# Low halves of 40 weight units: from a VectorE subtraction to a ScalarE negation plus an accumulating DMA

## The chip, the core and the metric

The kernel runs on one core of a Trainium2 chip. The metric is the device time of one execution in microseconds; lower is better. TensorE (PE) multiplies matrices, ScalarE (ACT) and VectorE (DVE) work elementwise, GpSimd (POOL) does a little arithmetic and issues some DMAs, SyncE (SP) issues the weight loads.

## The reference, cut to what matters

Two transformer-like layers over 256 tokens of width 2048, all in float32. The first is attention (differential attention and retention), cross-attention over a memory of 256 tokens and a gated feed-forward; the second is a hybrid of windowed attention and pooling. Nearly all work is in products of a 256-row activation with large weights:

```python
proj = h @ w_in[l]                       # 2048 x 7168
dq, dk, dv, rq, rk, rv, rg = split_cols(proj)
...
x = x + mixed @ w_o[l]
xq = (hx @ w_xq[l]); xk = (hm @ w_xk[l]); xv = (hm @ w_xv[l])
x = x + xo @ w_xo[l]
x = x + (jax.nn.silu(hf @ w_gate[l]) * (hf @ w_up[l])) @ w_down[l]
```

## The kernel before

**Units.** Every weight matrix is read once, as a stream of 128x1024 float32 tiles (512 KB), called `raw`. One such tile is one unit of a product (a few later ones are cut smaller). A product keeps float32 accuracy by splitting each operand into two parts: `hi`, the value rounded to the type that TensorE multiplies in one pass (float32r), and `lo`, the rest. A product is then made of three, hi·hi, hi·lo and lo·hi. `split_to` (L379 to L382) makes the two parts of a weight unit: ScalarE casts `raw` to `hi` (L381), VectorE subtracts, `lo = raw - hi` (L382).

**Matmuls.** There are two shapes of product. In layout "R" (`gemm_1k`) a unit holds one slice of 128 rows of the weight and is the moving operand: 12 matmuls with 512 columns each (L348, L349, L350), the second of which reads `lo`. In layout "T" (`gemm`) a unit holds two slices of 512 columns and is the stationary operand: 8 pairs of matmuls (L283 and L284, both through L353), the second of each pair reading `lo`. TensorE executes its matmuls in the order of the program.

**The stream.** `emit_items` walks a list of items made by `plan`. For a unit it takes a `hi` and a `lo` buffer (4 of each, `SPL_BUFS`), splits the unit, and then issues the load of the raw tile that comes six tiles later into the buffer just read (`RAW_BUFS = 6`, issued by SP at L230). `next_unit` is called ahead of the matmuls of unit u and emits the splits up to unit u + 3 (`LOOK = 3`); ahead of the last unit of a product it looks only two ahead, and `look_ahead` makes up for it in the middle of the evacuation. So the cast of unit u + 3 takes the buffer of unit u - 1, and can start when TensorE is done with unit u - 1. All engines work through their own instructions in the order of the program, so a cast also stands behind the ScalarE work that was emitted before it.

**Around it.** Between units `tick` emits one step of small jobs: softmax heads, transposes, evacuations. On POOL these are the power functions of the norms (L361) and the loads of the memory (L799).

**The stretch that the change touches** runs from the product `rv` (the retention values) to `xv1` (the last product of the cross-attention's values): rv, rg, o0, o1 (layout R, 16 units each), xk and xq in two halves each (layout T, 64 units), xv0 and xv1 (layout R, 16 each). That is 160 units, all 128x1024.

Of the kernel before, what the change touches and what calls it, by code (L numbers as in the profile page):

```python
# [9 lines left out]
F32 = mybir.dt.float32  # L10
F32R = mybir.dt.float32r
AF = mybir.ActivationFunctionType
ALU = mybir.AluOpType
# [106 lines left out]
class Builder:  # L120
# [113 lines left out]
    def emit_items(self, upto):  # L234
        while self.next_item <= min(upto, len(self.items) - 1):
            i = self.next_item
            job, c0, n, fn = self.items[i]
            raw = self.raw[job][:, c0 : c0 + n]
            if fn:
                fn(raw)  # L240
            else:
                hi = self.wpool.tile([P, n], F32R, tag="hi", name=f"hi{i}", bufs=SPL_BUFS)
                lo = self.wpool.tile([P, n], F32R, tag="lo", name=f"lo{i}", bufs=SPL_BUFS)
                for c in range(0, n, 256 if i == 0 else n):
                    w = slice(c, c + (256 if i == 0 else n))
                    self.split_to(raw[:, w], hi[:, w], lo[:, w])
                self.units[i] = (hi, lo)
            self.next_item += 1
            if c0 + n == 1024:
                del self.raw[job]  # L250
                self.emit_dma()
# [279 lines left out]
    def build(self):  # L531
        a = self.a
        w_in, w2 = a["w_in"][0], a["w_in_2"][0]
        G = {}

        def group(name, w, c0, ncol=1024, k0=0, nkt=KT, unit=None):
            G[name] = Gemm(name, w, k0, nkt, c0, ncol, unit or ncol)
            order.append(G[name])

        def wide(name, w, c0, ncol=1024, k0=0, nkt=KT):  # L540
            for i in range(ncol // 512):
                group(f"{name}.{i}", w, c0 + i * 512, 512, k0, nkt, 1024)

        order = []
        group("dq", w_in, 0)
        wide("dk", w_in, 1024)
        group("dv", w_in, 2048)
        wide("rqk", w_in, 3072)
        group("rv", w_in, 4096)
        group("rg", w_in, 5120)  # L550
        for c in range(2):
            group(f"o{c}", a["w_o"][0], c * 1024)
        for c in range(2):
            for n in ("xk", "xq"):
                wide(f"{n}{c}", a[f"w_{n}"][0], c * 1024)
        for n in ("xv", "xo"):
            for c in range(2):
                group(f"{n}{c}", a[f"w_{n}"][0], c * 1024)
        parts = ((0, 16), (16, 16), (32, 12))
        self.ff = []  # L560
        for pi, (k0, nk) in enumerate(parts):
            for i in range(nk // 4):
                for n in ("gate", "up"):
                    group(f"{n[0]}{pi}{i}", a[f"w_{n}"][0], (k0 + 4 * i) * P, 512, unit=1024)
            for c0, n in DOWN_COLS[pi == 2]:
                group(f"d{pi}{c0}", a["w_down"][0], c0, n, k0, nk)
            self.ff.append(nk)
        group("pu", w2, 2560)
        wide("gp", w2, 3584)
        wide("q", w2, 0)  # L570
        wide("kv", w2, 1024, 512)
        for c in range(4):
            if c == 2:
                wide("ga", w2, 1536)
            wide(f"m{c}", a["w_merge_2"][0], c * 1024)
        for c in range(4):
            wide(f"ba{c}", a["w_branch_attn_2"][0], c * 512, 512, 0, 8)
            wide(f"bp{c}", a["w_branch_pool_2"][0], c * 512, 512, 0, 8)
        for c0, n in OUT_COLS:
            group(f"out{c0}", a["w_out_2"][0], c0, n)  # L580

        ada = a["w_ada_2"][0]
        extras, todo = {}, []
        for k in range(KT):
            for c in range(0, 3 * D, 1024):
                src = ada[k * P : k * P + P, c : c + 1024].rearrange("p (b c) -> p b c", b=1)
                todo.append((src, self.ada_item(k, c)))
        hosts = []
        for g in order:
            if g.name[:2] in ("g0", "u0", "g1", "u1") or g.name in ("g20", "u20"):  # L590
                hosts += [(g.name, j) for j in HOST_W]
            elif g.name[:2] in ("d0", "d1"):
                hosts += [(g.name, j) for j in HOST_R]
        for i, ex in enumerate(todo):
            extras[hosts[i + 4]] = [ex]
        hosts = [(n, j) for n, js in SHIFT_HOSTS for j in js]
        for k in range(KT):
            extras[hosts[k]] = [(G["pu"].src[k], self.shift_item(k))]
        wp = a["w_pool_group_2"][0].rearrange("g (b p) d -> p (g b) d", p=P)
        for i in range(2):  # L600
            extras[("gp.0", 3 + i)] = [(wp[:, 4 * i : 4 * i + 4, :], self.pool_item(i))]
        wo = a["w_out_2"][0][:, OUT_REST:].rearrange("(k p) c -> p k c", p=P)
        for i in range(4):
            extras[("out0", 8 + 2 * i)] = [(wo[:, 4 * i : 4 * i + 4, :], self.out_item(i))]
        self.plan(order, extras)

        self.block1(G)
        self.ffn(G)
        self.block2(G)
        assert self.unit_no == len(self.unit_item)  # L610
        self.es.close()
# [1014 lines left out]
```

## Time and profile before

| | |
|---|---|
| time, median of 2 runs | 2114.75 us (2112.83 to 2116.67) |
| time of the profiled execution | 2116.45 us |
| its span (first to last instruction of the program) | 2114.6 us |
| PE busy | 2102.7 us, 99% |
| DVE busy | 1398.5 us, 66% |
| ACT busy | 1052.1 us, 50% |
| POOL busy | 80.9 us, 4% |
| bytes moved by DMA | 453.54 MB, mean 214 GB/s |

The span is what the profiler saw of the program; the time of the same execution is 1.85 us longer. Busy times are shares of the span. In the rows below, L381 is line 381 of the kernel; `out<-in` names tiles with their buffer numbers left out.

### The profile page before, as it was taken

Reading aid. Unit: us, or ns where it says so; the run is one execution under the profiler, and the core shown is the slowest. Engines: PE = TensorE matmul, PEld = TensorE weight load, DVE = VectorE, ACT = ScalarE, POOL = GpSimd, SP = SyncE. Lnnn points to the kernel's source line nnn. Section 1 sums busy time; section 2 is a strip of 40 time slices with the busy share of each in tenths; the row PEclk is TensorE's granted clock in tenths of the full one; section 3 lists DMA queues with packets and bytes.
Section 4 is the critical chain, followed back from the end, with each engine's and each line's share of the span. In section 5 each row is a group of like instructions: output and inputs, shape, how many; then the busy total and the mean of one; then the engine's idle time right before and its main releaser. Section 6 shows DMA issues by size and latency. Waiting matters only on the chain.

```text
span 2114.6 us, 30084 instructions
## 1 busy us (share of the span) xinstructions
PE 2102.7 (99%) x11582; PEld 1821.0 (86%) x11582; DVE 1398.5 (66%) x1762; ACT 1052.1 (50%) x1598; POOL 80.9 (4%) x97
## 2 busy tenths in 40 slices
PE   9999999999999999999999999999999999999998
PEld 9888888888888888888888888888898988888887
DVE  5556655665555557787777777877876766546764
ACT  5454555565444455444344443444755554655543
POOL 0200010000000000000000000000000000001300
PEclk9999999999999999999999999999999999999999
DMA  7755556555655567888888887768866556565562
GB/s 261 213 193 172 184 165 203 186 170 169 201 168 169 170 188 248 292 274 295 265 278 288 268 304 257 257 195 304 267 191 188 185 174 188 173 191 177 185 234 90
DMA packets 188527, 453.54 MB, mean 214 GB/s; under 512 B 14742, under 2 KB 23264, under 8 KB 188128
## 3 DMA queue, kind: packets, MB, share of 16 engines
q1 hardware_dynamic: 184992, 441.58, 64.3%
q0 software_dynamic: 3392, 10.06, 1.5%
q8 instruction: 90, 1.47, 0.3%
q14 instruction: 53, 0.43, 0.1%
HBM read 449.46 MB, written 4.22 MB: 215 GB/s over the span
## 4 chain that ended last, share of the span: by engine, by line
PE 98%; DMA 0%; issue 0%; DVE 0%; SPq 0%; ACT 0%; DVEq 0%; POOLq 0%; POOL 0%; ACTq 0%
PE acc L353 56%; PE acc L349 13%; PE acc L348 13%; PE acc L350 13%; PE m L353 1%; PE m L390 1%; PE m L349 1%; PE m L350 1%; PE m L348 1%; DMA raw<-in_w_in 0%; PE m L972 0%; PE m L1217 0%; DVE S L1342 0%; PE m L921 0%; SPq L228 0%
## 5 line engine op out<-in xcount | busy, mean ns | idle before, releaser
L382 DVE TENSOR_TENSOR lo<-raw,hi 128x1024 fp32r<-128x1024 f32 (+2 forms) x751 | 880.6, 1183 | 486.6 <-ACT hi L381 484.2
L353 PE MATMUL acc<-S,hi 128*128 128x512 f32 x3360 | 1186.4, 397 | 0.0
L381 ACT CAST hi<-raw 128x1024 fp32r<-128x1024 f32 (+2 forms) x751 | 748.0, 1010 | 526.9 <-PE acc L350 228.7
L353 PE MATMUL acc<-S,lo 128*128 128x256 f32 x3360 | 941.4, 280 | 0.0
L353 PEld LDWEIGHTS acc<-S,hi 128*128 128x128 f32 x3360 | 630.7, 188 | 150.3 <-issue 0.9
L353 PEld LDWEIGHTS acc<-S,lo 128*128 128x128 f32 x3360 | 634.4, 189 | 0.3
L348 PE MATMUL acc<-hi,S 128*128 128x512 f32 (+1 forms) x1088 | 422.1, 388 | 0.0
L349 PE MATMUL acc<-lo,S 128*128 128x512 f32 (+1 forms) x1088 | 417.0, 383 | 0.3 <-DVE lo L382 0.3
L350 PE MATMUL acc<-hi,S 128*128 128x512 f32 (+1 forms) x1088 | 417.3, 384 | 0.0
L350 PEld LDWEIGHTS acc<-hi,S 128*128 128x128 f32 x1088 | 204.4, 188 | 40.8
L349 PEld LDWEIGHTS acc<-lo,S 128*128 128x128 f32 x1088 | 204.6, 188 | 38.7 <-DVE lo L382 0.6
L348 PEld LDWEIGHTS acc<-hi,S 128*128 128x128 f32 x1088 | 204.5, 188 | 38.8
L343 DVE TENSOR_TENSOR S<-acc,S 128x256 f32<-128x256 f32 x136 | 54.0, 420 | 60.4 <-ACT S L342 60.3
L342 ACT COPY S<-acc 128x256 f32<-128x256 f32 x136 | 47.2, 377 | 85.4 <-PE acc L353 85.4
L624 DVE SCALAR_TENSOR_TENSOR S<-raw,ccol,S 128x1024 f32<-128x1024 f32 x60 | 76.7, 1278 | 0.0
L348 PE MATMUL acc<-S,hi 128*128 128x256 f32 x256 | 73.4, 287 | 0.6 <-ACT hi L381 0.6
L350 PE MATMUL acc<-S,lo 128*128 128x256 f32 x256 | 72.6, 284 | 0.9 <-DVE lo L382 0.9
L349 PE MATMUL acc<-S,hi 128*128 128x256 f32 x256 | 72.6, 284 | 0.4 <-DVE S L394 0.4
L350 PEld LDWEIGHTS acc<-S,lo 128*128 128x128 f32 x256 | 49.0, 192 | 1.3 <-DVE lo L382 1.3
L348 PEld LDWEIGHTS acc<-S,hi 128*128 128x128 f32 x256 | 49.1, 192 | 0.8 <-ACT hi L381 0.7
L349 PEld LDWEIGHTS acc<-S,hi 128*128 128x128 f32 x256 | 49.1, 192 | 0.7 <-DVE S L394 0.6
L381 ACT CAST S<-S 128x512 fp32r<-128x512 f32 x34 | 21.1, 621 | 50.5 <-DVE S L1050 48.5
(286 smaller groups left out, 1145.6 us busy)
## 6 DMA issues: line engine op xcount, KB each, us to landing
raw<-in_w_in SPq DMA_DIRECT2D x183, 512.0 KB, 4.4
raw<-in_w_ada SPq DMA_DIRECT2D x96, 512.0 KB, 4.7
raw<-in_w_gate SPq DMA_DIRECT2D x88, 512.0 KB, 4.9
raw<-in_w_up SPq DMA_DIRECT2D x88, 512.0 KB, 4.8
raw<-in_w_down SPq DMA_DIRECT2D x88, 512.0 KB, 5.5
raw<-in_w_merge SPq DMA_DIRECT2D x64, 512.0 KB, 4.3
raw<-in_w_o SPq DMA_DIRECT2D x32, 512.0 KB, 4.1
raw<-in_w_xk SPq DMA_DIRECT2D x32, 512.0 KB, 4.2
```

The costliest lines, as they stand in the source:

```text
L342: self.nc.scalar.copy(dst, bank[:, 1, :])
L343: self.nc.vector.tensor_tensor(dst, bank[:, 0, :], dst, op=ALU.add)
L348: mm(o, sh, mh, start=first, stop=False, skip_group_check=True)
L349: mm(o, sh, ml, start=False, stop=False, skip_group_check=True)
L350: mm(o, sl, mh, start=False, stop=last, skip_group_check=True)
L353: self.nc.tensor.matmul(o, l, r, start=start, stop=stop, skip_group_check=True)
L381: self.nc.scalar.copy(hi, src)
L382: self.nc.vector.tensor_tensor(lo, src, hi.bitcast(F32), op=ALU.subtract)
L390: nc.tensor.transpose(ps[:, i, t * P : t * P + P], rows(t)[:, i * P : i * P + P], self.ident)
L624: nc.vector.scalar_tensor_tensor(acc, raw, ck, acc, op0=ALU.mult, op1=ALU.add)
```

## The change

For every fourth item from the first unit of `rv` up to, and not including, the first of `xo0`, `lo` is made in another way. ScalarE casts `raw` to `hi` as before, then ScalarE writes `-hi` into `lo`, and then a DMA issued from POOL adds `raw` to `lo` in place. No other items lie in this part of the list, so these are 160 / 4 = 40 units. The VectorE subtraction of these units goes. The `raw` buffer of such a unit is read last by the DMA, and TensorE reads `lo` after the DMA has landed.

```diff
@@ emit_items
-                for c in range(0, n, 256 if i == 0 else n):
-                    w = slice(c, c + (256 if i == 0 else n))
-                    self.split_to(raw[:, w], hi[:, w], lo[:, w])
+                if i in self.added:
+                    self.nc.scalar.copy(hi, raw)
+                    self.nc.scalar.activation(lo, hi.bitcast(F32), AF.Copy, scale=-1.0)
+                    self.nc.gpsimd.dma_start(lo.bitcast(F32), raw, accum_op=ALU.add)
+                else:
+                    for c in range(0, n, 256 if i == 0 else n):
+                        w = slice(c, c + (256 if i == 0 else n))
+                        self.split_to(raw[:, w], hi[:, w], lo[:, w])
@@ build, after self.plan(order, extras)
+        first = self.unit_item[self.unit_name.index("rv")]
+        last = self.unit_item[self.unit_name.index("xo0")]
+        self.added = set(range(first, last, 4))
```

## Rows read from the trace of the kernel before

**Rows 1.** The page, part 1: busy us (share of the span) xinstructions.
```profile
PE 2102.7 (99%) x11582; PEld 1821.0 (86%) x11582; DVE 1398.5 (66%) x1762; ACT 1052.1 (50%) x1598; POOL 80.9 (4%) x97
```

**Rows 2.** The page, part 4: the chain that ended last, by engine.
```profile
PE 98%; DMA 0%; issue 0%; DVE 0%; SPq 0%; ACT 0%; DVEq 0%; POOLq 0%; POOL 0%; ACTq 0%
```

**Rows 3.** Busy time by stretch of the span, for the changed stretch.
```profile
core 0: us, PE busy (x) PEld busy (x) DVE busy (x) ACT busy (x) POOL busy (x), PEclk, DMA share, GB/s
...
201.43:674.59 473.16, 472.95 (x2451) 403.12 (x2449) 275.72 (x376) 243.58 (x399) 14.25 (x16) 1.00 0.56 178
```

**Rows 4.** The view of waits, PE alone, from 201 to 675 us.
```profile
PE m L862 <- DVE C L857: 0.2, 1, 0.2
```

**Rows 5.** Groups by line and shape: busy us, mean ns | idle before.
```profile
L382 DVE TENSOR_TENSOR lo<-raw,hi 128x1024 fp32r<-128x1024 f32 x691 | 845.8, 1234 | 470.2 <-ACT hi L381 467.7
...
L381 ACT CAST hi<-raw 128x512 fp32r<-128x512 f32 x40 | 24.2, 618 | 15.0 <-DVE lo L382 7.4 <-PE acc L350 6.3 <-DVE XR L1203 0.8
...
L512 ACT ACTIVATE J<-XR 128x512 f32<-128x512 f32 x24 | 15.2, 633 | 0.2
```

**Rows 6.** Groups by line, ACT alone, from 190 to 675 us.
```profile
L381 ACT CAST hi<-raw 128x1024 fp32r<-128x1024 f32 x161 | 166.9, 1050 | 102.5 <-PE acc L350 61.0 <-PE acc L353 38.7 <-issue 1.4
```

**Rows 7.** Timeline, ACT and PE (start us, us): cast of a unit, matmul reading its lo.
```profile
192.03 1.05 ACT L381 CAST hi<-raw 128x1024 fp32r<-128x1024 f32 x1 [1.72 <-PE acc L353]
201.85 0.40 PE L349 MATMUL acc<-lo,S 128*128 128x512 f32 x1
...
210.66 3.88 ACT L381 CAST hi<-raw 128x1024 fp32r<-128x1024 f32 x4
213.21 0.40 PE L349 MATMUL acc<-lo,S 128*128 128x512 f32 x1
...
481.77 1.05 ACT L381 CAST hi<-raw 128x1024 fp32r<-128x1024 f32 x1 [1.72 <-PE acc L353]
490.24 0.28 PE L353 MATMUL acc<-S,lo 128*128 128x256 f32 x1
...
618.64 1.04 ACT L381 CAST hi<-raw 128x1024 fp32r<-128x1024 f32 x1
625.45 0.39 PE L349 MATMUL acc<-lo,S 128*128 128x512 f32 x1
...
666.63 1.05 ACT L381 CAST hi<-raw 128x1024 fp32r<-128x1024 f32 x1 [1.67 <-PE acc L350]
674.81 0.39 PE L349 MATMUL acc<-lo,S 128*128 128x512 f32 x1
```

**Rows 8.** Timeline, ACT and POOL: a DMA issue on POOL that waited for ScalarE.
```profile
355.16 0.19 ACT L809 ACTIVATION_READ_ACCUMULATOR J<-A 128x1 f32 x1
...
355.64 0.72 POOL L799 DMA_DIRECT2D A<-in_mem  x1 [42.25 <-ACT J L809]
```

**Rows 9.** DMA issues: engine op xcount, KB each, median us from issue to landing.
```profile
raw<-in_w_xv SPq DMA_DIRECT2D x32, 512.0 KB, 4.5
...
A<-in_mem POOLq DMA_DIRECT2D x8, 256.0 KB, 4.3
...
adaB<-gaterow POOLq DMA_DIRECT2D x1, 1024.0 KB, 6.2
gf<-in_norm_f_g POOLq DMA_DIRECT2D x1, 1024.0 KB, 7.7
...
c<-c_ret POOLq DMA_DIRECT2D x1, 512.0 KB, 5.6
```

**Rows 10.** The view of one tile, raw: its loads.
```profile
DMA to landing us min/median/max: 2.8/4.6/9.2
```

**Rows 11.** The view of waits, SP alone: waited for, us in total, times, longest.
```profile
SPq L230 <- DVE lo L382: 1175.4, 596, 8.0
```

**Rows 12.** Groups by line, POOL alone, from 190 to 675 us.
```profile
L361 POOL TENSOR_TENSOR rs<-sm,mhalf 128x2 f32<-128x2 f32 x7 | 7.8, 1116 | 145.1 <-DVE sm L359 145.1
L799 POOL DMA_DIRECT2D A<-in_mem x8 | 5.8, 730 | 61.4 <-ACT J L809 61.4
```

## The prediction

> **What bounds the kernel now.** I read the shares of busy time first, then the chain that ended last, then the changed stretch alone. TensorE is busy 2102.7 of 2114.6 us [rows 1] and makes up 98% of the chain [rows 2]. The stretch that the change touches is tighter still: between 201.43 and 674.59 us PE is busy 472.95 of 473.16 us [rows 3], and the view of waits finds one PE wait in it, of 0.2 us [rows 4]. So nothing can be won here by making VectorE lighter; what counts is whether the new way of making `lo` is done when TensorE wants it. If it isn't, PE stalls, and each microsecond of stall moves the end by one, since no other engine's slack can give it back.
>
> The next thing to read is the time that a unit has. Its cast waits mostly for PE [rows 6], that is for its buffers, which TensorE gives back when it is done with the unit four before. From there it is three units until its own matmuls, and the second of these reads `lo`. I matched the 40 casts with that matmul: the first is 192.03 to 201.85 us (9.82), the last 666.63 to 674.81 us (8.18), the first and the last of 40 pairs [rows 7]. An ordinary window is three units long: 8.47 us in layout T (481.77 to 490.24), 8.18 us in layout R. A cast that stood behind other ScalarE work has less: 6.81 us (618.64 to 625.45), in the worst case 2.55 us (210.66 to 213.21) [rows 7]. The 40 windows in classes: 4 under 5.1 us, sum 16.8; 10 of 6.1 to 7.5, sum 66.3; 14 of 8.1 to 8.7, sum 116.7; 12 longer, of 8.8 to 12.6, the shortest of them 8.83, 9.13 and 9.17.
>
> **What is removed.** 40 VectorE subtractions of 1.234 us [rows 5], 49 us of an engine that is busy 276 of 473 us there [rows 3]. Worth nothing: PE didn't wait for them. With them a `lo` was ready about 1.05 + 1.23 = 2.3 us after the start of its cast, so some 5 to 6 us of the window were spare. The change spends these.
>
> **What is added on ScalarE.** 40 negations over 128x1024. The cast of that size takes 1.050 us [rows 6]; at 128x512 an activation takes 633 ns beside the cast's 618 [rows 5]; so I take 1.05 us. ACT goes from 243.6 to some 286 us of 473 [rows 3], 60%, so as a load it is hidden by ACT's idle time. In the queue the negation stands ahead of the next cast, which starts a unit (2.7 to 2.8 us) later, and ahead of evacuations and softmax steps, which move by up to 1.05 us, less than a unit; I cost that at nothing. As a link of the chain it counts in full.
>
> **What is added on POOL.** 40 DMA issues, each waiting for the negation. A POOL issue that waited for ScalarE started 0.29 us after it: 355.16 + 0.19 = 355.35, then 355.64 [rows 8]. Queued behind such a wait on POOL are the power functions and the loads of the memory, 16 instructions of 0.7 to 1.6 us in the stretch with hundreds of idle microseconds around them [rows 12]. They were emitted for the same stage of the program and their readers come several steps later; I cost their delay at nothing. If that cover were gone, each could cost up to the 2.1 us that cast and negation take.
>
> **What is moved.** The SP load of the raw tile six further on waits today for the subtraction [rows 11] and will wait for the landing, about 6 us later; the loads behind it on SP wait too, then go out in a bunch. A raw load lands 2.8 to 9.2 us after issue, 4.6 in the median [rows 10]. With C for the time from the cast to the landing, the held load can go at C. The cast that needs it comes six units later, or, if PE has stalled for `lo` on the way, no earlier than C plus three units, C + 8.2 us. So a median load is covered by 3.6 us and only the slowest would show. I cost it at nothing. Other loads in flight while the sum is made are few, because SP is held.
>
> **The length of the DMA** is the unknown, since no accumulating DMA is in the trace. The nearest rows [rows 9]: on POOL 256 KB in 4.3 us, 512 KB in 5.6 us (that one among other small loads), 1024 KB in 6.2 and 7.7 us; on SP 512 KB in 4.5 us. The new DMA writes 512 KB and reads 1024 KB, the old `lo` and `raw`. Bounds: 4.3 us, if reading on chip makes up for the second operand, and 7.7 us, if it goes like the slower 1024 KB row; 10 us if the two reads and the write of each row wait for one another, which no row here shows. It writes what the 5.6 us row writes and reads what the 1024 KB rows write (mean 6.95), so I take the middle of these, 6.3 us.
>
> The Trainium skill, "Collectives: The Full Stack", Part 3 (the bandwidth ceiling), says that an add inside a DMA costs no time for the addition itself but takes two source reads, which halves the rate against a copy; no run here shows it so far, and it speaks for the upper half of these rows.
>
> **The sum.** The chain is cast 1.05 + negation 1.05 + hand-off to POOL 0.29 + DMA 6.3 + start of the waiting matmul 0.05 = 8.74 us. A window shorter than that stalls PE by the difference: the 4 shortest 4 x 8.74 - 16.8 = 18.2 us, the next 10 87.4 - 66.3 = 21.1 us, the 14 ordinary ones 122.4 - 116.7 = 5.7 us; together 45 us. A stall doesn't add up from unit to unit, because the next marked unit's window begins anew three units before it. On the profiled execution's 2116.45 us that is 2161; the median lies 1.7 us below that execution, so 2160 us. That is +2.1%, just at what a measurement of this kernel tells from no change (2%, 42 us). The same sum for other lengths: DMA 4.3 us, +13; 5.6, +30; 6.95, +64; 7.7, +89; 10, +177 us. The sum reaches 42 us at a DMA of 6.2 us.
>
> **Rivals.**
> Hidden, and so not slower: the DMA lands in under 5 us, as the 256 KB row and SP's 512 KB row do [rows 9], the ordinary windows hold it, and only late casts stall. It decides from 6.2 us downwards; at 4.3 us it gives 2128. For it: both ends are on chip, and SP, held, leaves the queues empty. Against it: POOL's 512 KB row took 5.6 us, and this one reads twice that.
> The Trainium skill, "DMA: Bandwidth & Descriptors", Anatomy of one DMA — SWDGE (gpsimd) path, gives such a DMA 2.0 us plus its bytes at 436 GB/s; for 1 MB of reads that is an estimate of 4.4 us, near this rival, but by it POOL's 256 KB would take 2.6 us and the trace has 4.3, so I lean on the rows.
> Slow adding: 7.7 us and more, each ordinary window stalls too, +89 to +177, that is 2204 to 2292. Nothing in the trace excludes it.
> Held raw loads: if the bunch of loads behind a held one lands late (the longest raw load took 9.2 us [rows 10], against 8.2 us of cover), casts wait for raw, up to 1 us at each of 40, on top of the forecast: 2200.
> No effect or a gain: PE waits for nothing in the stretch [rows 4], so the most to win there is 0.2 us: 2115.
>
> **Chances.** Forecast family (DMA of 5 to 7.7 us, +20 to +89) 0.53; hidden 0.17; slow adding 0.23; held loads 0.05; no effect 0.02. Within 2% are hidden, no effect and the part of the forecast family under 6.2 us (0.23): 0.42. Slower by over 2%: the rest of the family 0.30, slow adding and held loads, 0.58, of which I take 0.02 for faster by over 2%, for what I haven't seen, as 42 us cannot come out of a stretch without waits; 0.56 is left. The range leaves out a tenth at each side: 2124 (DMA under about 4 us) to 2262 (DMA over 9.2 us). The likeliest case's own range is 2135 to 2204.
>
> **What the profile after would show.** PE busy about the same 2103 us of a longer span; PE idle in the stretch, put down to the DMA into `lo`, 20 to 35 times, longest after the late casts. POOL with 40 more DMA issues; their time to landing is the number that decides, read from the list of issues. VectorE 49 us lighter, ScalarE 42 us heavier. SP's waits for `lo` in part replaced by waits for the DMA. The prediction is wrong if that landing time lies outside 5 to 7.7 us, if the issue on POOL itself is much longer than the 0.73 us of the loads there now [rows 12], or if stalls bring the granted clock down from 1.00 [rows 3].

## The result, and the profile after

The changed kernel takes 2151.6 us (2150.06 to 2153.13, 2 runs) against 2114.75: ratio 1.017 [1.0149, 1.019], 36.9 us more. It lies in the range (2124 to 2262) and 8 us under the forecast of 2160. The loss is clear of noise, but by 2% it counts as no change, a class that had 0.42; I had given 0.56 to slower by over 2%.

The kernel before itself runs at either of two levels, near 2112 or near 2116 us, so each version below is given by its ratio to runs of before made beside it.

The page after, part 1 (busy us, share of the span, instructions); the span is 2151.4 us:

```profile
PE 2113.4 (98%) x11582; PEld 1826.6 (85%) x11582; DVE 1351.7 (63%) x1722; ACT 1094.0 (51%) x1638; POOL 116.7 (5%) x137
```

Against [rows 1] this line already divides the loss. The span grew by 2151.4 - 2114.6 = 36.8 us. PE is busy 2113.4 - 2102.7 = 10.7 us longer with the same 11582 matmuls, so some of them ran slower; and its idle time went from 11.9 to 38.0 us, +26.1. DVE is 46.8 us lighter and ACT 41.9 us heavier, and PE's waits below name neither of them for the loss.

Where PE was idle shows in the view of waits (waited for: us in total, times, longest):

```profile
PE acc L358 <- DMA lo<-raw: 14.6, 7, 2.7
PE acc L354 <- DMA lo<-raw: 9.7, 7, 4.6
PE m L395 <- DMA A<-in_mem: 2.4, 2, 1.8
PE m L358 <- DVE mhalf L424: 1.1, 1, 1.1
```

L354 and L358 hold the matmuls that read `lo`, in layout R and in layout T. They waited 14 times, 24.3 us in all, where before had 0.2 us of PE waits of any kind in the stretch [rows 4]. Another 2.4 us went to loads of the memory, which share POOL's queue with the new DMAs; the last row stands in before too.

The rest shows in busy time by stretch (start and end, length, busy time of PE with its matmuls, PEld, DVE, ACT, POOL, then the granted clock, the DMA share and GB/s). First before, then after, both cut at the same matmuls: from the first of rv to the last of xv1, and from some 1795 us of before to the end.

```profile
201.43:686.83 485.40, 485.19 (x2505) 413.25 (x2503) 281.97 (x383) 249.68 (x407) 14.25 (x16) 1.00 0.56 178
...
1795.00:2114.60 319.60, 311.27 (x1748) 270.25 (x1746) 191.12 (x239) 166.22 (x269) 30.04 (x18) 0.99 0.56 176
```

```profile
201.13:726.83 525.70, 499.01 (x2505) 420.16 (x2504) 235.61 (x344) 290.00 (x446) 49.10 (x55) 0.98 0.72 204
...
1835.53:2151.40 315.87, 307.45 (x1748) 268.49 (x1746) 191.69 (x239) 166.10 (x269) 29.84 (x18) 0.99 0.56 178
```

The changed stretch is 40.3 us longer, not 36.8. The end of the kernel, which the change doesn't touch, is 3.7 us shorter, because the two profiled executions ran it at different paces (the last section returns to this). In the stretch PE's idle time grew by 26.5 us, which are the waits above, and its busy time by 13.8 us.

The largest part of the busy time is the clock:

```profile
217.10:223.80 6.70, 6.13 (x16) 4.87 (x17) 1.93 (x2) 0.39 (x2) 0.00 (x0) 0.50 0.91 311
...
497.00:500.30 3.30, 1.08 (x7) 0.72 (x6) 1.23 (x1) 1.05 (x1) 0.00 (x0) 1.00 0.86 216
500.40:503.70 3.30, 3.30 (x11) 2.75 (x11) 0.00 (x0) 0.00 (x0) 0.00 (x0) 0.50 0.84 258
...
582.00:585.60 3.60, 1.63 (x10) 1.17 (x9) 1.23 (x1) 1.05 (x1) 0.00 (x0) 1.00 0.83 196
585.80:589.00 3.20, 3.20 (x11) 2.72 (x11) 0.00 (x0) 0.80 (x1) 0.00 (x0) 0.50 0.95 320
```

It was 1.00 throughout the stretch before [rows 3]. Now it falls to 0.50, the lower of its two levels (1.2 GHz), five times: first for 6.8 us, beginning 0.6 us before the end of a stall of 4.6 us, then four times for 3.4 us, each 0.1 to 1.3 us behind a stall of 2.0 to 2.7 us. Of these 20.5 us PE was busy for 19.8, and half of that is lost, 9.9 us. Of the other 3.9 us of busy time some 2.5 belong to the 16 waits: the view counts a wait from the modelled end of the matmul ahead of it, so a little of each lies in the busy time. At the first one below the two starts are 4.99 us apart (212.68 and 217.67) where 0.23 us are usual, so 4.76 us are lost and 4.60 counted. The last 1.4 us I can't assign.

The links of the chain, from the view of the tile `lo` (ns min/median/max, first and last start) and from the groups of POOL (busy us, mean ns | idle before):

```profile
L246 ACT ACTIVATE lo<-hi x40: 1057/1062/1064, 192.8 to 707.8; 128x1024 fp32r<-128x1024 f32 x40
...
DMA to landing us min/median/max: 4.5/4.9/6.2
```

```profile
L247 POOL DMA_DIRECT2D lo<-raw x40 | 34.9, 873 | 425.5 <-ACT lo L246 378.1 <-PE acc L355 29.2 <-PE acc L354 12.5
```

And two marked units in the timeline (start us, us, engine, what [idle before <- releaser]), the one with the shortest window and one from the class of 6.1 to 7.5 us:

```profile
210.36 1.04 ACT L245 CAST hi<-raw 128x1024 fp32r<-128x1024 f32 x1
211.43 1.06 ACT L246 ACTIVATE lo<-hi 128x1024 fp32r<-128x1024 f32 x1
212.80 0.88 POOL L247 DMA_DIRECT2D lo<-raw  x1 [17.65 <-ACT lo L246]
217.67 0.80 PE L354 MATMUL acc<-lo,S 128*128 128x512 f32 x1 [4.60 <-DMA lo<-raw]
...
464.40 1.04 ACT L245 CAST hi<-raw 128x1024 fp32r<-128x1024 f32 x1
465.48 1.06 ACT L246 ACTIVATE lo<-hi 128x1024 fp32r<-128x1024 f32 x1
...
466.84 0.90 POOL L247 DMA_DIRECT2D lo<-raw  x1 [1.95 <-ACT lo L246]
472.94 0.52 PE L358 MATMUL acc<-S,lo 128*128 128x256 f32 x1 [2.02 <-DMA lo<-raw]
```

The first is the late cast of [rows 7], at 210.66 there; the DMA takes 4.8 us from issue to landing, and PE stands for 4.6 of them. The second had a window of 6.4 us before; its chain is 2.44 us to the issue and 6.1 us for the DMA, and PE stands for 2.0. With a DMA of 4.5 us it would still have stood for some 0.5.

Matched unit by unit with the windows before, the 14 stalls are the 4 windows under 5.1 us, 9 of the 10 from 6.1 to 7.5, and a single one of the 14 ordinary ones (0.6 us, at a landing of 6.2 us).

### The profile page after: what moved, and what is told of

Read it like the earlier page. It is cut to its first block, busy times and chain, and to the rows that moved or that the text cites. A ratio compares the mean times of both kernels' runs of the same rounds, so it can differ in the third digit from the quotient of the medians.

```text
span 2151.4 us, 30170 instructions
## 1 busy us (share of the span) xinstructions
PE 2113.4 (98%) x11582; PEld 1826.6 (85%) x11582; DVE 1351.7 (63%) x1722; ACT 1094.0 (51%) x1638; POOL 116.7 (5%) x137
## 4 chain that ended last, share of the span: by engine, by line
PE 69%; DMA 1%; ACT 0%; DVE 0%; issue 0%; DVEq 0%; POOLq 0%; POOL 0%; ACTq 0%
PE acc L358 43%; PE acc L354 8%; PE acc L355 8%; PE acc L353 8%; DMA lo<-raw 1%; PE m L354 0%; PE m L355 0%; PE m L353 0%; PE m L980 0%; PE m L1225 0%; PE m L395 0%; DVE lo L387 0%; PE m L358 0%; ACT hi L386 0%; DVE S L1350 0%
## 5 line engine op out<-in xcount | busy, mean ns | idle before, releaser
L358 PE MATMUL acc<-S,hi 128*128 128x512 f32 x3360 | 1189.6, 398 | 0.0
L387 DVE TENSOR_TENSOR lo<-raw,hi 128x1024 fp32r<-128x1024 f32 (+2 forms) x711 | 833.6, 1182 | 545.3 <-ACT hi L386 543.2
L358 PE MATMUL acc<-S,lo 128*128 128x256 f32 x3360 | 943.2, 281 | 14.6 <-DMA lo<-raw 14.6
L386 ACT CAST hi<-raw 128x1024 fp32r<-128x1024 f32 (+2 forms) x711 | 707.6, 1008 | 473.3 <-PE acc L355 202.4
L358 PEld LDWEIGHTS acc<-S,hi 128*128 128x128 f32 x3360 | 633.3, 188 | 149.6 <-issue 0.9
L358 PEld LDWEIGHTS acc<-S,lo 128*128 128x128 f32 x3360 | 636.7, 190 | 17.1 <-DMA lo<-raw 16.8
L354 PE MATMUL acc<-lo,S 128*128 128x512 f32 (+1 forms) x1088 | 419.0, 385 | 10.1 <-DMA lo<-raw 9.7
L354 PEld LDWEIGHTS acc<-lo,S 128*128 128x128 f32 x1088 | 205.3, 189 | 51.6 <-DMA lo<-raw 12.6
L354 PE MATMUL acc<-S,hi 128*128 128x256 f32 x256 | 72.6, 284 | 0.9 <-DVE S L399 0.9
L245 ACT CAST hi<-raw 128x1024 fp32r<-128x1024 f32 x40 | 42.0, 1049 | 40.3 <-PE acc L358 24.3
L247 POOL DMA_DIRECT2D lo<-raw x40 | 34.9, 873 | 425.5 <-ACT lo L246 378.1
L354 PEld LDWEIGHTS acc<-S,hi 128*128 128x128 f32 x256 | 49.1, 192 | 1.2 <-DVE S L399 1.1
```

The lines of the kernel that those rows point to most:

```text
L245: self.nc.scalar.copy(hi, raw)
L247: self.nc.gpsimd.dma_start(lo.bitcast(F32), raw, accum_op=ALU.add)
L354: mm(o, sh, ml, start=False, stop=False, skip_group_check=True)
L358: self.nc.tensor.matmul(o, l, r, start=start, stop=stop, skip_group_check=True)
L386: self.nc.scalar.copy(hi, src)
L387: self.nc.vector.tensor_tensor(lo, src, hi.bitcast(F32), op=ALU.subtract)
```

## Experiments

**Theory.** PE waits for `lo` because cast, negation and DMA in a row are longer than the window of some units; the rest is what these stalls bring with them. Rivals: the negation delays other ScalarE work; the DMA traffic or the longer-held raw buffers cost the time, whoever waits.

**The negation without the DMA.** VectorE adds `raw` to the negated `lo`.

```diff
-                    self.nc.gpsimd.dma_start(lo.bitcast(F32), raw, accum_op=ALU.add)
+                    self.nc.vector.tensor_tensor(lo, raw, lo.bitcast(F32), op=ALU.add)
```

> The negation on ScalarE stays, the accumulating DMA goes: VectorE adds raw to the negated value instead. Theory A (TensorE waits for a low half that the DMA lands late): a low half is ready 1.05 + 1.06 + 1.23 = 3.4 us after the start of its cast, inside every ordinary window, so no stall on a low half, clock 1.00 in the stretch, 2113 to 2118 us. Rival B (the 42 us of extra ScalarE work push casts and evacuations late): 10 us or more of the 37 stay, 2125 us or more.

Measured: 2113.29 us, ratio 1.0004 [0.9994, 1.0013]. One PE wait for such a `lo` is left, of 0.7 us. So the 40 negations cost nothing that shows as a load on ScalarE.

**The DMA without anyone waiting for it.** `lo` is made as before by the subtraction, and 40 DMAs of the same size are issued from POOL onto the raw tile after its last use; they change nothing that is read later. The raw buffer is held by them as in the change. `side_copy` is the same without the addition.

```diff
-                    self.nc.scalar.copy(hi, raw)
-                    self.nc.scalar.activation(lo, hi.bitcast(F32), AF.Copy, scale=-1.0)
-                    self.nc.gpsimd.dma_start(lo.bitcast(F32), raw, accum_op=ALU.add)
+                    self.split_to(raw, hi, lo)
+                    self.nc.gpsimd.dma_start(raw, hi.bitcast(F32), accum_op=ALU.add)   # side_copy: no accum_op
```

> The 40 units are split by VectorE as in the kernel before, and then an accumulating DMA of the same size adds hi onto the raw tile, which nothing reads; its raw buffer is held until it lands, as in the change (about 2.3 + 0.3 + 4.9 = 7.5 us after the start of the cast). There is no negation. The output is not touched. Theory A: nobody on TensorE waits for these DMAs, so 2113 to 2119 us, with time to landing near 4.9 us and POOL as busy as in the change. Rival B (the DMA's traffic, the held raw buffers or POOL's queue cost the time): 2125 to 2150 us.

> As side_dma, but the DMA is a plain copy of hi onto the dead raw tile, without the addition. If the addition costs through its second read, the share of the software queue falls to about half of the change's and the median time to landing from 4.9 to some 3.4 to 4.0 us; if the addition is free in time, the landing stays at 4.7 to 4.9 us. The time of the kernel is 2113 to 2119 us either way.

Measured: 2117.74 us, ratio 1.0026 [1.0015, 1.0037], +5.6 us, for the accumulating one; 2116.84 us in a single run, +4.7, for the copy (2.5 of them at the end of the kernel, by its pace there). PE waits 3.3 and 1.8 us for the memory's loads, and never for the `lo` of these units; in `side_dma` the clock also falls once to 0.50, for 3.4 us, 1.4 us behind the longer of the two waits (2.1 us). So traffic and held buffers without a wait for `lo` make at most 6 of the 37 us, nearly all of it by way of the memory's loads; what comes with the wait makes the rest. The two also show what the addition costs the DMA (issue rows: operation, count, KB each, median us to landing; first the accumulating one):

```profile
raw<-hi POOLq DMA_DIRECT2D x40, 512.0 KB, 5.7
...
q0 software_dynamic: 9152, 31.03, 7.3%
```

```profile
raw<-hi POOLq DMA_DIRECT2D x40, 512.0 KB, 3.5
...
q0 software_dynamic: 9152, 31.03, 4.1%
```

The queue's rows give packets, MB and the share of 16 engines' span. In before the queue had 3392 packets and 1.5% (31.7 us of the span), so the 40 DMAs are 5760 packets. An accumulating packet took (0.073 x 2116.0 - 31.7) x 16 / 5760 = 0.34 us, a plain one (0.041 x 2115.1 - 31.7) x 16 / 5760 = 0.15 us: about twice.

**The windows.** The same 40 sums at other units of the group of four: `offset1` starts one item later, `offset3` three.

```diff
-        self.added = set(range(first, last, 4))
+        self.added = set(range(first + 1, last, 4))   # offset3: first + 3
```

> The 40 units one place further along: every fourth unit from the second of rv on. Same work, same DMAs. In the trace of the kernel before, the windows of these units are mostly longer: with a chain of 7.35 us five of them are too short, by 4.6 us in all, with 7.8 us eight, by 7.8 us. Theory A: 5 to 12 us over the kernel before, with the wait for the memory's loads, 2117 to 2125 us. Rival B (a fixed cost for each DMA): 37 us over, as before, 2147 to 2154 us.

> The 40 units three places along: every fourth unit from the fourth of rv on. In the trace of the kernel before, eight of these units have windows of 4 to 5.4 us: with a chain of 7.35 us, eleven are too short, by 23.5 us in all, with 7.8 us by 29 us, eight of them by 2 to 3.9 us. Theory A: 24 to 30 us of stalls and 5 to 13 us of clock, 2141 to 2156 us, about the changed kernel's time. Rival B: 2147 to 2154 us as well; so this run tells apart nothing alone, but beside offset1 it shows whether the place decides.

Measured: 2138.77 us, 1.0122 [1.0107, 1.0137], and 2155.02 us, 1.0203 [1.0186, 1.022]. PE's waits for `lo` are 14.7 and 22.8 us. Which units are taken matters, as the theory says. But I had worked out offset1 from its windows alone and it came out higher, at +26.3 us instead of 5 to 12: its landings reach 9.5 us, so windows don't decide by themselves. And offset3 waits no longer for `lo` than the changed kernel (23.8 us in `again`, below), yet takes 5.4 us more. It has one long wait for the memory,

```profile
PE m L395 <- DMA A<-in_mem: 5.6, 1, 5.6
```

and 27.3 us at the lower clock against 17.1 in `again`.

**A shorter chain.** `-hi` is made straight from `raw`, ahead of the cast, so that the DMA can go 1.05 us earlier.

```diff
-                    self.nc.scalar.copy(hi, raw)
-                    self.nc.scalar.activation(lo, hi.bitcast(F32), AF.Copy, scale=-1.0)
+                    self.nc.scalar.activation(lo, raw, AF.Copy, scale=-1.0)
                     self.nc.gpsimd.dma_start(lo.bitcast(F32), raw, accum_op=ALU.add)
+                    self.nc.scalar.copy(hi, raw)
```

> ScalarE writes minus the rounded raw value into lo straight from raw and first, POOL's DMA follows, and the cast to hi comes after; so the same work with a chain shorter by one ScalarE instruction, 1.05 us. Theory A (each stall is the part of the chain that sticks out of the window, and the clock falls behind stalls over 2 us): the 14 measured stalls on low halves, each 1.05 us shorter, leave some 14 of 24 us, of them one over 2 us; with the wait for the memory's loads (2.4 us) and one clock period, 16 to 22 us over the kernel before, 2127 to 2134 us. Rival B (cost by DMA or by ScalarE work, not by lateness): no change from the changed kernel, 2147 to 2154 us.

Measured: 2144.2 us, 1.0149 [1.0134, 1.0164], 5.5 us less than the changed kernel beside it (2149.66, below), a third of what I expected. Why, the views of waits, of the tile `lo` and the timeline show:

```profile
PE acc L358 <- DMA lo<-raw: 14.3, 7, 3.7
PE acc L354 <- DMA lo<-raw: 5.2, 4, 3.3
```

```profile
DMA to landing us min/median/max: 4.5/5.5/8.6
```

```profile
464.11 1.05 ACT L245 ACTIVATE lo<-raw 128x1024 fp32r<-128x1024 f32 x1
...
465.46 0.90 POOL L246 DMA_DIRECT2D lo<-raw  x1 [0.86 <-ACT lo L245]
...
472.15 0.38 PE L358 MATMUL acc<-S,lo 128*128 128x256 f32 x1 [1.53 <-DMA lo<-raw]
```

Late casts gain as expected (9.7 to 5.2 us in layout R). In layout T the DMA starts earlier but takes longer: 6.6 us at this unit, median 5.5 instead of 4.9. The reason suspected here was raw loads in flight. The trace bears it out over all 40 units: the 16 sums that landed within 4.9 us had other loads in flight beside them for 0.4 to 3.4 us (added up over the loads), the 15 that took 6.6 us and more for 4.1 to 25.1 us. The wait for the memory's loads grew too, from 2.4 to 4.1 us.

**Raw loads kept away from the sum.** The load that belongs to the unit before a marked one is put behind a 4-byte DMA on SP that reads `lo`, so it goes out only after the sum has landed. `hold_neg` adds the edit of neg_first, `hold_neg_off` also the start one item later.

```diff
             if c0 + n == 1024:
                 del self.raw[job]
-                self.emit_dma()
+                if i in self.added:
+                    mark = self.sml.tile([P, 1], F32, tag="mark", name=f"mark{i}", bufs=1)
+                    self.nc.sync.dma_start(mark[0:1, :], self.units[i][1].bitcast(F32)[0:1, 0:1])
+                if i + 1 in self.added:
+                    self.held = 1
+                else:
+                    for _ in range(1 + getattr(self, "held", 0)):
+                        self.emit_dma()
+                    self.held = 0
```

> The changed kernel, but SP keeps the raw load that belongs to the unit ahead of a marked one back until the accumulating DMA has landed (a DMA of 4 bytes that reads the low half stands ahead of it in SP's order). Theory A with contention (the accumulating DMA takes 4.5 to 5 us alone and 5.5 to 9.5 us beside raw loads issued shortly before it): landing 4.5 to 5.3 us in nearly all 40, the stalls of the middle units of the T products fall by about 1 us each, stalls on low halves 16 to 20 instead of 24 us, 2138 to 2147 us. Rival B (landing varies for another reason, as its place in the order or POOL's issue): landing spreads to 6 us as before and the time stays at 2149 to 2153 us. Rival D (held loads make casts wait for raw): waits for raw loads show and the time is over 2153 us.

> As hold, and with the negation ahead of the cast, as in neg_first. There the chain got 1.05 us shorter, but the DMA then ran beside raw loads and took 5.5 us in the median instead of 5.0. Theory A with contention: now it takes 4.5 to 5.3 us, the chain is 6.2 us, and stalls on low halves fall to 8 to 12 us, with the memory's loads and one or two clock periods 2126 to 2134 us. Rival B: as neg_first, 2142 to 2147 us.

> As hold_neg, with the units one place further along, as in offset1, where by the trace of the kernel before one window alone is shorter than 6.25 us, by about 1 us. Theory A with contention: stalls on low halves under 4 us, no or one clock period, the rest is the wait for the memory's loads, 2114 to 2120 us, the same as the kernel before within 0.3%. Rival B (some cost sticks to each DMA): 2125 us or more.

Measured: hold 2149.27 us, 1.016 [1.0143, 1.0176]; hold_neg 2138.44, 1.0103 [1.0088, 1.0118]; hold_neg_off 2134.25, 1.0084 [1.0068, 1.0099]; that is +33.0, +22.2 and +18.0 us. The unit of the timeline above, in the changed kernel (SP's row, and the tile's landing from 460 to 476 us) and in hold:

```profile
465.79 8.52 SPq L230 DMA_DIRECT2D raw<-in_w_xq  x5
...
DMA to landing us min/median/max: 6.1/6.1/6.1
```

```profile
464.56 0.90 POOL L247 DMA_DIRECT2D lo<-raw  x1 [1.95 <-ACT lo L246]
...
469.13 0.60 SPq L258 DMA_DIRECT2D mark<-lo  x1
469.82 1.92 SPq L230 DMA_DIRECT2D raw<-in_w_xq  x4
...
474.81 0.90 POOL L247 DMA_DIRECT2D lo<-raw  x1 [7.81 <-ACT lo L246]
...
DMA to landing us min/median/max: 4.6/5.1/5.7
```

Of the five loads in the first row two, issued at 465.79 and 468.76 us, land while the sum runs or just behind it (469.39 and 474.18). With the loads kept back, this unit's sum lands in 4.6 us instead of 6.1. So contention with the raw loads is shown for it. PE still stands 0.8 us for it, as the window is short. But the four loads let go at 469.82 run into the next sum at 474.81, which takes 5.7 us, and over the 40 units the median stays at 4.9 with a longest of 8.6; in the combinations the median even rises to 5.8 and 6.9 us. That is why hold alone gained only 4 us, and the two combinations fell short of what I expected; by their times hold and hold_neg_off lie with their rivals. The combinations' PE waits for `lo` are 11.9 and 9.5 us. 4 to 6 us of what the three still cost are in none of the views of waits and not in the clock; by the count from start to start about half of that belongs to the waits, and 2 to 3 us I can't assign.

**The clock.** PE is given work in the nine longest stalls on `lo`: 103 matmuls with zeros as the stationary operand (`fill`; its expectation counts 102), or 92 with a zero as the moving operand (`fill2`), which add nothing to the result. `again` is the changed kernel once more.

```diff
+FILL = {68: 21, 140: 8, 148: 10, 156: 10, 164: 10, 172: 13, 180: 10, 188: 10, 196: 11}
...
                     self.mm(self.flat(banks[b]), wh[:, i, c], x.both(k), first, False)
+                    if b == 0 and i == 0:
+                        for _ in range(FILL.get(self.unit_no - 1, 0)):
+                            self.mm(self.flat(banks[b]), self.zeros, x.both(k), False, False)
```

(layout T; the same in layout R between the first and the second matmul of the unit)

> The changed kernel once more, beside the kernel before on the same chip as the three that follow. From its first runs (2150.1 and 2153.1 us): 2147 to 2154 us, ratio 1.015 to 1.019, stalls of some 24 us on low halves, and several half-clock periods of 3.4 us or more behind the longest of them, not always the same ones.

> The changed kernel, but in the 9 units with the longest stalls TensorE gets 8 to 21 matmuls of a zero stationary tile (102 in all, adding zero to the bank) ahead of the matmul that waits for the low half, about as long as its stall (0.22 us each). Theory A with the clock as a second term (the stalls bring the granted clock to half after some of them, 20 us at half clock, 10 us lost): stalls are now covered by work of the same length, the clock stays at 1.00 in the stretch and the time falls by about 10 us to 2138 to 2145. Rival C (the half-clock periods have nothing to do with the stalls): the periods stay and the time stays at 2148 to 2156.

> The clock once more. As fill, with 92 matmuls in the 9 longest stalls instead of 102, and made from a real stationary tile and a zero column read 512 times over, so that no constant is added and no tile of the kernel is moved. In fill the half-clock periods were gone from the stretch and the stretch was 6 to 10 us shorter than in the changed kernel, but the last part of the kernel ran 3.7 us longer, so that the time was nearly the same. Theory A (clock lost behind stalls, some 10 us): clock 1.00 in the stretch, 2138 to 2145 us. Rival C (the clock periods cost nothing, or come anyway): 2147 to 2153 us.

Measured: again 2149.66 us, 1.0176 [1.0161, 1.0191], +37.1; fill 2149.0, 1.0175 [1.0158, 1.0192], +36.8; fill2 2148.13, 1.0151 [1.0136, 1.0166], +31.9. The stretch, first in again, then in fill, then in fill2, and behind it in each the part from 1830 us on, which the change doesn't touch:

```profile
200.00:715.00 515.00, 488.82 (x2472) 411.86 (x2471) 230.96 (x338) 286.41 (x443) 49.00 (x55) 0.98 0.72 205
...
1830.00:2000.00 170.00, 170.00 (x988) 149.90 (x986) 100.72 (x119) 100.49 (x157) 10.72 (x6) 1.00 0.58 186
```

```profile
200.00:715.00 515.00, 510.46 (x2604) 431.09 (x2604) 234.13 (x342) 289.07 (x446) 49.00 (x55) 1.00 0.73 208
...
1830.00:2000.00 170.00, 170.00 (x970) 147.60 (x969) 99.87 (x116) 98.96 (x155) 10.97 (x6) 1.00 0.59 183
```

```profile
200.00:715.00 515.00, 508.27 (x2593) 429.06 (x2592) 234.11 (x342) 288.80 (x446) 49.01 (x55) 1.00 0.73 208
...
1830.00:2000.00 170.00, 170.00 (x970) 147.60 (x969) 99.88 (x116) 99.14 (x155) 10.98 (x6) 1.00 0.59 183
```

With the filling the clock is 1.00. From its start at 200 us to the end of the last product of xv1 the stretch is 40.0 and 36.5 us longer than before in the two profiles of the changed kernel, and 30.3 and 30.4 us in the filled ones: the clock costs 6 to 10 us there, as 20.5 and 17.1 us at half the clock suggest. fill2 shows it in the whole time (5 us less than again). fill doesn't, because its profiled execution went at the slower pace from 1830 us on (970 matmuls in 170 us against 988 in again, both at clock 1.00) while nearly all runs of before beside it were at 2112 us; for fill2 all those runs were at 2116 us. That the whole time of fill didn't fall is therefore no evidence against the clock. By their times alone both runs lie where I had put the rival, not at 2138 to 2145 us; what decides is the clock of 1.00 and the 6 to 10 us less in the stretch. The filling occupies the stalls, it doesn't end them, so what is left of the loss is the waits.

No version beat the kernel before.

## Why the prediction was right, and where it wasn't

**What bounds the kernel**: right. TensorE had no wait to lose, so a lighter VectorE gave nothing and every stall moved the end. But not by one microsecond for each of its own: 26.7 us of waits made the stretch 40.3 us longer, with the clock as the largest other part.

**ScalarE**: right. The negation takes 1.062 us against 1.05 taken, free as a load (vector_add), full as a link: with the chain shorter by one such step the waits in layout R fell from 9.7 to 5.2 us (neg_first).

**POOL**: the hand-off is 0.31 us (211.43 + 1.06 = 212.49, then 212.80) against 0.29, the issue 0.873 us against 0.73. That the delay of its neighbours costs nothing was wrong by 2.4 us: the memory's loads land 5.7 us after issue in the median instead of 4.3 [rows 9], and PE waited for them twice. Nor was 2.1 us the most that a neighbour could lose. POOL stands from the moment it reaches the new DMA, before the cast has begun, here for 5.88 us; the memory's last load stood behind it, and went out 7.2 us after the one ahead of it instead of 4.6:

```profile
383.59 0.72 POOL L807 DMA_DIRECT2D A<-in_mem  x1 [3.83 <-ACT J L817]
390.18 0.92 POOL L247 DMA_DIRECT2D lo<-raw  x1 [5.88 <-ACT lo L246]
390.76 1.08 POOL L807 DMA_DIRECT2D A<-in_mem  x1
```

**Held raw loads**: as such at nothing, right. Raw loads land in 2.6/4.7/10.0 us against [rows 10], and no ScalarE cast in the stretch waits for one. SP's waits moved from the subtraction [rows 11] to the DMA, as foretold:

```profile
SPq L230 <- DVE lo L387: 1089.6, 533, 8.5
SPq L230 <- DMA lo<-raw: 155.4, 40, 11.3
```

What failed is the sentence behind it, that other loads in flight are few because SP is held. SP holds only the loads behind the marked one; those ahead of it in SP's order run beside the sum (two of them at the unit with 6.1 against 4.6 us), and a bunch let go after one sum can run into the next (shown in hold).

**The length of the DMA**: the step that was mis-sized. I took 6.3 us; it is 4.9 in the median and 4.5 at the least, just outside the 5 to 7.7 that I had named as the bounds of being right. By my own sign the prediction was wrong here, and "under 5 us" belonged to the rival "hidden". The 512 KB row on SP (4.5) was nearer than the 1024 KB rows on POOL that I leaned on; those differ from the new DMA in size and in where they read, and which of the two matters no run separates. The addition does cost: side_dma and side_copy show 0.34 against 0.15 us a packet, 5.7 against 3.5 us to landing. The rule of the Trainium skill on two source reads ("Collectives: The Full Stack", Part 3) agrees with that; that it is the second read no run shows by itself. And the estimate of 4.4 us from the Trainium skill ("DMA: Bandwidth & Descriptors", Anatomy of one DMA — SWDGE (gpsimd) path), which I had set aside, was nearer to the 4.5 us of an undisturbed one than the 6.3 us that I took.

**The sum**: 8.74 us for the chain, 45 us of stalls, 20 to 35 of them. With 4.9 us the same sum gives a chain of 7.34 us and 4 x 7.34 - 16.8 + 10 x 7.34 - 66.3 = 19.7 us; measured are 24.3 us in 14 stalls. The windows were the right way to count. What is missing are the landings over 4.9 us, up to 6.2, which a sum with one length can't have: with each unit's own landing and its window before, the sum is 26.7 us, which is what the 14 waits come to when each is counted from start to start (26.5).

**What I left out**: the clock. I named a fall of it as something that would make the prediction wrong, and gave it no price; it cost about 10 us. So by two of the signs that I had named, the landing time and the clock, the prediction was wrong, and it was luck that the forecast came within 8 us: it had 45 us of stalls instead of 24.3, and nothing for the clock and the memory's loads instead of some 12.

**The rivals**: "hidden" has the length of the DMA about right (under 5 us) and the ordinary windows do hold 4.9 us, all but one; it fails where the windows of 6.1 to 7.5 us are too short for it, and where loads stretch the sum. Slow adding and held loads didn't come, and no gain did.

Open are three things: why some stalls of 2.0 to 2.7 us were followed by the lower clock and others of 2.1 to 2.3 not, so that "stalls over 2 us", as I had it for neg_first, is no rule; the 2 to 3 us of the hold versions; and what sets the two paces of the part from 1830 us on. A look-ahead of one unit more, which would lengthen every window by a unit, some 2.7 us, wasn't tried; it takes one more `hi` and `lo` buffer (8 KB a partition).

## What to carry to other kernels

A link put on an engine that is idle is free as a load and still counts in full as a step of the chain: compare the length of the chain with the window of each single unit, not with the mean, for it is the few late ones that stall. A DMA's length depends on what else is in flight beside it; starting it earlier or holding other loads back only helps as far as it doesn't put it, or the next one, beside a bunch. And a stall of TensorE may have to be paid a second time, in matmuls at the lower clock behind it.

## What the hardware showed that I had not expected

- A single stall of 2.0 to 4.6 us in a stretch that is otherwise full brought, five times, 3.4 or 6.8 us at a granted clock of 0.50; in the R layout the matmuls then start 0.42 to 0.43 us apart, against 0.23 at 1.00. Three other stalls, of 2.1 to 2.3 us, did not.

```profile
218.26 0.63 PE L355 MATMUL acc<-hi,S 128*128 128x512 f32 x1
218.69 0.63 PE L353 MATMUL acc<-hi,S 128*128 128x512 f32 x1
219.11 0.63 PE L354 MATMUL acc<-lo,S 128*128 128x512 f32 x1
```

- The same accumulating DMA of 512 KB took 4.5 us with little or no load beside it and up to 9.5 us among raw loads of another queue (offset1). The Trainium skill ("DMA: Bandwidth & Descriptors", Queues, rings and completion order) says that an engine takes turns between the queues that have work for it, packet by packet; the 6.1 against 4.6 us of one unit with and without SP's loads agree with that.
- The addition lengthens the issue on POOL too: 871 ns in the mean against 543 for the plain copy.
- At one granted clock (1.00) the same part of the program runs at two paces, whatever the kernel: 964 matmuls in 170 us in before against 983 in vector_add, and 970 in fill and fill2 against 988 in again.
